# Neighbourhood attention on one core: the layout of attention's output in DRAM, and the order of the transposes of the probabilities

## The chip, the core and the metric

The kernel runs on one core of a Trainium2 chip. The metric is the device time of one execution in microseconds (us); less is better. Three runs of the kernel before took 992.84, 990.8 and 990.86 us, so its median is 990.86 us.

## The reference, cut to what matters

One encoder layer over 2048 tokens (32 rows by 64 columns) of 1024 numbers, all float32:

```
h = rmsnorm(x, norm_0)
q, k, v, gate = split(h @ w_in_0, 4)             # 16 heads of 64
# every query sees 8 rows by 16 columns of keys around it
s = q @ k.T / 8 + bias(rpb_0, row and column offset)
o = softmax(s) @ v
x = x + (o * silu(gate)) @ w_out_0
out = rmsnorm(x, norm_f)
```

## The kernel before, in words

TensorE does the matmuls, and each large product is split into three passes over a high and a low part of the operands. Four stages follow each other on it.

- `stage_one` and `stage_two` project the first and second half of the tokens to q, k, v and the gate. Seven products in place of eight are formed for each block (the method of Strassen), and the results go to DRAM (`qd`, `kd`, `vd`, `sgd`).
- Attention: a loop over 32 cycles, one for each pair of heads p (0 to 7) and quarter of the tokens T (0 to 3), in the order of the list `order` (L1214): T = 1 and 0 for all eight pairs first, then T = 2 and 3.
- `outputs` multiplies the first four row tiles (128 tokens each) by `w_out`, in small pieces between attention's steps.
- `rows_by_seven` multiplies the other twelve row tiles by `w_out`, again by seven products.

One cycle of attention works on two "quads" of columns. `scores` (L1311) makes 64 small matmuls for each quad into two PSUM banks s0 and s1. VectorE adds the bias and takes the row minimum (L1320), ScalarE takes the exponent (L1327), and `normalise` multiplies by the reciprocal of the sum, on GpSimd, ScalarE and VectorE (L1343, L1341, L1339). The probabilities of a cycle lie in eight tiles `X[quad, half, s]`. In the next cycle `turns` (L1347) transposes them on TensorE: 48 transposes of 64 rows, for three blocks b of 120 columns, into two PSUM banks ph0 and ph1 for each block. As soon as a block is done, ScalarE copies ph0 and VectorE copies ph1 to the tile `pta` (L1367, L1365). Then come the scores of the present cycle, then `values` (L1384), which multiplies `pta` by the values `vt` into the bank o, and L1388 multiplies o by the gate into `og`. Between these steps `feed` puts matmuls of the last projections (L384 to L388) or of `outputs` (L1586 to L1590), so that TensorE has work while the other engines do the softmax.

Eight PSUM banks are handed out in turn to whoever asks next; a matmul that opens a bank waits until the bank's last reader is done.

All loads and stores but a few go through one queue, that of SyncE (SP). Eight semaphores take turns there, so an issue waits until the transfer eight issues before it has landed; the transfers are worked off by 16 DMA engines in the order of issue. In each cycle SP issues the loads of the next cycle's keys `kt` (L1232), queries `q` (L1241), values `vt` (L1250), gates `sgt` (L1255) and bias tables `em` (L1269), and stores of the projections. When each is due is written in the code as a count of matmuls (`store`, `later_loads`).

Attention's output passes through DRAM. The tile `og` is 128 partitions (the two heads' 64 dimensions) by 512 tokens, four row tiles i of 128. There is one DRAM tile `ogd[T]` for each quarter, in which each partition holds 16 KB, laid out as row tile, pair, token:

```
ogd = [dram.tile([128, 4, NP, 128], F32, name=f"ogd{T}") for T in range(4)]      # L70
nc.sync.dma_start(ogd[T][:, :, p], og.rearrange("p (i q) -> p i q", i=4))        # L1391
nc.sync.dma_start(t, ogd[T][:, i])                                               # L1418
nc.sync.dma_start(A[m, f]..., ogd[T][:, i, 4 * half:4 * half + 4])               # L1642
```

The 32 stores (L1391, 256 KB each) write four runs of 512 B in each partition. The four loads of `load_og` (L1418, tile `ograw`, 512 KB) read one run of 4 KB, for `outputs`. The 24 loads of `load_rows_of` (L1642, tile `raw`, 256 KB) read one run of 2 KB, for `rows_by_seven`.

In `rows_by_seven` the first three groups of row tiles lead: their products 1 and 2 (six products of 12 matmuls) come first, then product 6 of group 0, which is the first to use the part T2 of `w_out`. T2 is loaded into the tiles `woh` and `wol` by `land_T2` (eight loads of 256 KB, L1610).

Of the kernel before, what the change touches and what calls it, by code (L numbers as in the profile page):

```python
# [24 lines left out]
NP = H // 2  # L25
# [6 lines left out]
RES_BUFS, RES_EARLY = 3, 1  # L32
PLAIN = 4

FRAME, TALL = [0, 4, 12, 17], 15
# [26 lines left out]
def build(ctx, tc, x, xr, xt, wg, bias, w_out, n0, nf, out):  # L62
# [1150 lines left out]
    stored_at = {}  # L1213
    order = [(p, T) for p in range(NP) for T in (1, 0)] + [(p, T) for p in range(NP - 2) for T in (2, 3)]  # L1214
    order += [(NP - 2, 2), (NP - 1, 2), (NP - 1, 3), (NP - 2, 3)]
# [3 lines left out]
    def load_k(p, T):  # L1219
        r0, r1, more = PARTS[T]  # L1220
        base = 12 * (T > 1)
        a, b = r0 * GW, r1 * GW + more
        must(*[("k", p, c) for c in range(a // 512, (b + 511) // 512)])

        def keys():
            if T in (1, 2):
                khalf.clear()
                KT[p, T // 2] = (kp([128, 2048], F32, "kt") if p % 2 == 0 else mkp([128, 1536], F32, "kt"))[:, :1344]
            t = KT[p, T // 2]
            if T == 2:  # L1230
                nc.gpsimd.memset(t[:, 1280:1288], 0.0)
            nc.sync.dma_start(t[:, a - base * GW:b - base * GW], kd[p][:, a:b])  # L1232

        return keys
# [24 lines left out]

    def load_bias(p, T):  # L1260
        fs = []
        kind = BRINGS[T]
        w = 2 * WIDE * TABLES[kind][2]
        EM[p, T // 2, kind] = []
        for quad in range(2):
            t = mp([128, 512], F32, "em")[:, :w]
            EM[p, T // 2, kind].append([t[:, :w // 2], t[:, w // 2:]])
# [30 lines left out]
    def scores(i, between=None):  # L1298
# [16 lines left out]
        for half, (u, n) in enumerate(HALF_ROWS[T]):  # L1315
            xs_ = [by_column(X[quad, half, s], HALF_ROWS[T][half]) for s in range(2)]
            table = EM[p, T // 2, kinds_of[T][half]][quad]
# [29 lines left out]
    def turns(m):  # L1347
# [3 lines left out]
        t = PT[m].rearrange("p (s b n c) -> p b s n c", s=2, b=3, c=64)  # L1351
        for b in range(3):
            ph = [bank(512, f"ph{h}") for h in range(2)]
            at = (2 - b) * k
            for quad in range(2):
                for half in range(2):
                    for s in range(2):
                        for h in range(2):
                            q = slice(64 * h, 64 * h + 64)
                            o = s * 256 + half * 128 + quad * 64  # L1360
                            nc.tensor.transpose(ph[h][:k, o:o + 64], X[quad, half, s][q, at:at + k], ident[q, q])  # L1361
            for h in range(2):
                o, i_ = t[:k, b, :, h::2], ph[h][:k].rearrange("p (s n c) -> p s n c", s=2, c=64)
                if h:
# [6 lines left out]
    def values(m):  # L1371
# [18 lines left out]
        def keep():  # L1390
            nc.sync.dma_start(ogd[T][:, :, p], og.rearrange("p (i q) -> p i q", i=4))  # L1391
            written.add(("og", p, T))
            stored_at[p, T] = clock[0]
# [20 lines left out]
    def load_og(n):  # L1414
        T, i = divmod(n, 4)
        must(*[("og", p, T) for p in range(NP)])
        G[n] = t = wp([128, NK, 128], F32, "ograw")
        nc.sync.dma_start(t, ogd[T][:, i])  # L1418

# [217 lines left out]
    def load_rows_of(m, f, home=None):  # L1637
# [3 lines left out]
        A[m, f] = (home or raw)([128, 512], F32, "raw")  # L1641
        nc.sync.dma_start(A[m, f].rearrange("p (k q) -> p k q", k=4), ogd[T][:, i, 4 * half:4 * half + 4])  # L1642

# [108 lines left out]
    dense, end_of_it = 13.5, 24  # L1752
    amount = [dense] * 25
    first = 16
# [3 lines left out]
    HEAD = 5  # L1758
    amount += [(96 * (12 - len(units_two)) + 48 * PLAIN - sum(amount) - first - end_of_it) / (cycles - 25)] * (cycles - 25) + [end_of_it - 6]
    fill = projections()  # L1760
# [29 lines left out]
    def begin(m):  # L1790
# [11 lines left out]
        if m + 1 < cycles:  # L1802
            nx = order[m + 1]
            later_loads([load_q(*nx), load_k(*nx)], 7, 5)
            later_loads(load_bias(*nx), 3, 1.5)

    stage_one()
# [93 lines left out]
```

## Time and profile before

| | |
|---|---|
| median of three runs | 990.86 us |
| the profiled execution's own time | 991.77 us |
| its span, first to last instruction | 989.8 us |
| TensorE clock granted | 0.998 of full |
| bytes moved by DMA | 227.89 MB in 149228 packets |
| DMA queue of SP | 146096 packets, 71.0% of 16 engines' span |

The page names engines PE (TensorE matmuls), PEld (TensorE weight loads), DVE (VectorE), ACT (ScalarE), POOL (GpSimd) and SP (SyncE, with "q" for its queue). A row of the timeline gives the start and the length in us, engine, line, operation, tile written <- tiles read, the number of instructions merged, and in brackets the idle time before with what ended it. A row of the waits gives who waited for whom: the total in us, how often, and the longest. A row of the table of windows gives the busy time of each engine in a stretch, the granted clock, the share of the 16 DMA engines that was busy, and what they moved in GB/s. PE counts as busy while matmuls overlap, so 39 of 40 slices read 9 tenths or more.

### The profile page before, as it was taken

The numbers are of one execution on the slowest core, as the hardware profiler recorded it, in microseconds if no ns is written. First come the engines' busy times: TensorE is split into PE (matmuls) and PEld (weight loads), VectorE is DVE, ScalarE is ACT, GpSimd is POOL, SyncE is SP. The second block draws the span as 40 slices with busy tenths as digits, with TensorE's granted clock in tenths as the row PEclk, the third lists the DMA queues.
The fourth block names the chain that finished last, engine by engine and source line by source line (L and its number), as shares of the span: only waits on it lengthen the run. The fifth ranks groups of instructions, "written<-read, shape, count | busy, mean of one in ns | idle before, by whom it ended". The sixth has DMA issues, their size and how long they took to land.

```text
span 989.8 us, 22264 instructions
## 1 busy us (share of the span) xinstructions
PE 979.6 (99%) x8172; PEld 797.4 (81%) x8172; DVE 757.3 (77%) x1703; ACT 532.5 (54%) x1310; POOL 148.1 (15%) x396
## 2 busy tenths in 40 slices
PE   9999999999999999999999999999999999999997
PEld 7888888888788888888888777778778777888886
DVE  5899888988565876766776577778878878877866
ACT  7773245465435342333433377677778776653443
POOL 0000001232100000000000033333333332311110
PEclk9999999999999999999999999999999999999999
DMA  8943547777957936657455899988999988997754
GB/s 287 334 131 104 197 130 251 250 224 253 350 179 216 293 117 183 206 165 241 166 184 188 229 275 278 270 260 265 296 287 294 286 227 265 304 369 188 204 148 117
DMA packets 149228, 227.89 MB, mean 230 GB/s; under 512 B 13312, under 2 KB 65792, under 8 KB 149120
## 3 DMA queue, kind: packets, MB, share of 16 engines
q1 hardware_dynamic: 146096, 221.37, 71.0%
q0 software_dynamic: 2592, 4.72, 2.8%
q8 instruction: 64, 1.05, 0.4%
q10 hardware_dynamic: 432, 0.40, 0.1%
q14 instruction: 44, 0.36, 0.1%
HBM read 160.37 MB, written 66.06 MB: 229 GB/s over the span
## 4 chain that ended last, share of the span: by engine, by line
PE 95%; DMA 3%; ACT 1%; DVE 1%; issue 0%; SPq 0%; ACTq 0%
PE pp L440 40%; PE pv L606 13%; PE py L1681 12%; PE o L1384 7%; PE s L1311 5%; PE ph L1361 4%; PE pv L721 2%; PE pp L384 2%; PE pp L388 2%; PE pp L386 2%; DMA kt<-kd 2%; PE po L1586 1%; PE po L1590 1%; PE po L1588 1%; DMA xr<-in_x_dram 1%; ACT x L1327 1%
## 5 line engine op out<-in xcount | busy, mean ns | idle before, releaser
L440 PE MATMUL pp<-h,f 128*128 128x512 f32 x576 | 185.3, 389 | 0.0
L440 PE MATMUL pp<-t,f 128*128 128x512 f32 x702 | 171.4, 389 | 0.0
L440 PEld LDWEIGHTS pp<-t,f 128*128 128x128 f32 x702 | 131.7, 188 | 27.6 <-DVE u L453 0.2
L1327 ACT ACTIVATE x<-x,st 128x253 f32<-128x253 f32 (+1 forms) x256 | 125.1, 496 | 32.9 <-DVE st L1320 32.9
L440 PEld LDWEIGHTS pp<-h,f 128*128 128x128 f32 x576 | 108.1, 188 | 22.6
L440 PE MATMUL pp<-l,f 128*128 128x512 f32 x288 | 112.1, 389 | 0.0
L1343 POOL TENSOR_SCALAR x<-x,st 128x253 f32<-128x253 f32 (+1 forms) x160 | 78.5, 510 | 130.5 <-DVE st L1332 127.1
L1320 DVE CUSTOM_DVE_ANT_0 x<-s,em 128x253 f32<-128x253 f32 (+1 forms) x256 | 87.3, 398 | 6.6 <-issue 4.5
L423 DVE TENSOR_TENSOR f<-raw,f 128x512 fp32r<-128x512 f32 x105 | 75.8, 727 | 20.0 <-ACT f L422 19.9
L1384 PEld LDWEIGHTS o<-pta,vt 120*64 120x64 f32 x1152 | 70.0, 137 | 18.4 <-issue 12.0
L1384 PE MATMUL o<-pta,vt 120*64 120x192 f32 (+2 forms) x1152 | 84.1, 299 | 0.0
L422 ACT ACTIVATE f<-raw 128x512 fp32r<-128x512 f32 x105 | 63.7, 623 | 36.2 <-DVE raw L429 22.0
L1365 DVE COPY pta<-ph 120x512 f32<-120x512 f32 x96 | 60.3, 684 | 13.6 <-PE ph L1361 13.1
L1367 ACT ACTIVATE pta<-ph 120x512 f32<-120x512 f32 x96 | 50.5, 599 | 33.8 <-PE ph L1361 33.6
L440 PEld LDWEIGHTS pp<-l,f 128*128 128x128 f32 x288 | 54.1, 188 | 11.2
L1681 PE MATMUL py<-woh,f 128*128 128x512 f32 x192 | 60.9, 390 | 0.0
L1311 PE MATMUL s<-kt,q 64*32 64x253 f32 (+1 forms) x2048 | 58.7, 362 | 2.2 <-DMA kt<-kd 1.7
L1361 PEld LDWEIGHTS ph<-ident,x 64*120 64x120 f32 x1536 | 47.6, 135 | 11.3 <-issue 10.6
L606 PE MATMUL pv<-wh,t 128*128 128x512 f32 x176 | 56.4, 390 | 0.1
L440 PE MATMUL pp<-sixths,f 128*128 128x512 f32 x198 | 52.7, 389 | 0.0
L461 POOL TENSOR_TENSOR tmp<-tmp,rb 128x512 f32<-128x512 f32 x18 | 28.4, 1580 | 158.0 <-DVE tmp L458 138.3
L1361 PE MATMUL ph<-ident,x 64*120 64x64 f32 x1536 | 52.0, 221 | 0.0
(230 smaller groups left out, 1883.7 us busy)
## 6 DMA issues: line engine op xcount, KB each, us to landing
raw<-in_wg_dram SPq DMA_DIRECT2D x124, 256.0 KB
vt<-vd SPq DMA_DIRECT2D x32, 480.0 KB
row<-in_xr_dram SPq DMA_DIRECT2D x32, 256.0 KB
vd<-v SPq DMA_DIRECT2D x32, 256.0 KB
sgd<-sg SPq DMA_DIRECT2D x32, 256.0 KB
q<-qd SPq DMA_DIRECT2D x32, 256.0 KB
sgt<-sgd SPq DMA_DIRECT2D x32, 256.0 KB
ogd<-og SPq DMA_DIRECT2D x32, 256.0 KB
```

The source lines that it names most:

```text
L422: nc.scalar.activation(t[:, 0], src, AF.Copy)
L423: nc.vector.tensor_tensor(t[:, 1], src, t[:, 0].bitcast(F32), OP.subtract)
L440: nc.tensor.matmul(B[n, P], t[:, int(m == 2), c], x[k][int(m == 1)], start=P in (1, 6, 5) and k == 0 and m == 0, stop=k == 3 and m == 2, s ...
L606: nc.tensor.matmul(p, a[:, o], b, start=P in (1, 6, 5) and k == 0 and m == 0, stop=k == 3 and m == 2, skip_group_check=True)
L1311: nc.tensor.matmul(places[half, s][h * 32:h * 32 + 32], qt[a, g * 64 + half * 32:g * 64 + half * 32 + 32], kt[a, o:o + n * GW].rearrange(" ...
L1320: nc.vector.tensor_tensor_reduce(xs_[s], places[half, s].rearrange("p (r c) -> p c r", c=WIDE), table[s].rearrange("p (c r) -> p c r", c=W ...
L1327: nc.scalar.activation(xs_[s], xs_[s], AF.Exp, bias=st[:, o:o + 1], scale=-1.0, accum_out=st[:, 4 + o:5 + o])
L1343: nc.gpsimd.tensor_scalar(t, t, st[:, o:o + 1], 1.0, op0=OP.mult, op1=OP.mult)
L1361: nc.tensor.transpose(ph[h][:k, o:o + 64], X[quad, half, s][q, at:at + k], ident[q, q])
L1365: nc.vector.tensor_copy(o, i_)
L1384: nc.tensor.matmul(o[s * 64:s * 64 + 64, g0 * 64:g1 * 64], vt[:k, strip, s * 64:s * 64 + 64], moving, start=strip == 0, stop=strip == 7, s ...
L1681: nc.tensor.matmul(B[m, P], t[:, a, c], b, start=P in (1, 6, 5) and k == 0 and i == 0, stop=k == 3 and i == 2, skip_group_check=True)
```

## The change

Two things are changed; what else the diff holds does nothing at the value that it sets.

1. `ogd[T]` is laid out as pair, row tile, token. A store then writes one run of 2 KB in each partition, a load of `load_og` reads eight runs of 512 B, and a load of `load_rows_of` reads four runs of 512 B.
2. `turns` no longer does both quads of a block in a row. With (block, quad), the order is (0,0), (1,0), (0,1), (2,0), (1,1), (2,1), and a block is copied after its quad 1. The pairs of banks are asked for in the same order as before, but those of blocks 1 and 2 are opened eight transposes earlier, and blocks 0 and 1 are copied eight transposes later.

The constant `SHARED` is 0. With it the list `order`, the bias tables loaded, their keys and the tile that holds each pair's keys come out as before, and every row of SyncE, VectorE, ScalarE and GpSimd stands where it stood.

```
+SHARED = 0
...
-    ogd = [dram.tile([128, 4, NP, 128], F32, name=f"ogd{T}") for T in range(4)]
+    ogd = [dram.tile([128, NP, 4, 128], F32, name=f"ogd{T}") for T in range(4)]
...
-        for b in range(3):
-            ph = [bank(512, f"ph{h}") for h in range(2)]
+        ph = {}
+        for b, quad in ((0, 0), (1, 0), (0, 1), (2, 0), (1, 1), (2, 1)):
+            if quad == 0:
+                ph[b] = [bank(512, f"ph{h}") for h in range(2)]
             at = (2 - b) * k
-            for quad in range(2):
-                for half in range(2):
-                    for s in range(2):
-                        for h in range(2):
...
-                            nc.tensor.transpose(ph[h][:k, o:o + 64], X[quad, half, s][q, at:at + k], ident[q, q])
+            for half in range(2):
+                for s in range(2):
+                    for h in range(2):
...
+                        nc.tensor.transpose(ph[b][h][:k, o:o + 64], X[quad, half, s][q, at:at + k], ident[q, q])
+            if quad == 0:
+                continue
...
-            nc.sync.dma_start(ogd[T][:, :, p], og.rearrange("p (i q) -> p i q", i=4))
+            nc.sync.dma_start(ogd[T][:, p], og.rearrange("p (i q) -> p i q", i=4))
...
-        nc.sync.dma_start(t, ogd[T][:, i])
+        nc.sync.dma_start(t, ogd[T][:, :, i])
...
-        nc.sync.dma_start(A[m, f].rearrange("p (k q) -> p k q", k=4), ogd[T][:, i, 4 * half:4 * half + 4])
+        nc.sync.dma_start(A[m, f].rearrange("p (k q) -> p k q", k=4), ogd[T][:, 4 * half:4 * half + 4, i])
```

Where the rows move is TensorE in each of the 32 turns. Before, in turn 10, counted from 0 (tile numbers kept; ph0_7214 and ph1_7215 are the banks of block 0, ph0_7234 and ph1_7235 those of block 1; x tiles up to number 5193 and from 5199 to 5201 are quad 0), from the seventh transpose on:

```order
L1361 MATMUL ph0_7214<-ident_163,x1_5201 120x64 [waits Pool_49]
L1361 MATMUL ph1_7215<-ident_163,x1_5201 120x64
L1361 MATMUL ph0_7214<-ident_163,x0_5195 120x64 [waits Pool_49]
L1361 MATMUL ph1_7215<-ident_163,x0_5195 120x64
L1361 MATMUL ph0_7214<-ident_163,x1_5197 120x64 [waits Activation_49]
L1361 MATMUL ph1_7215<-ident_163,x1_5197 120x64
L1361 MATMUL ph0_7214<-ident_163,x0_5203 120x64 [waits DVE_49]
L1361 MATMUL ph1_7215<-ident_163,x0_5203 120x64
L1361 MATMUL ph0_7214<-ident_163,x1_5205 120x64 [waits DVE_49]
L1361 MATMUL ph1_7215<-ident_163,x1_5205 120x64
L1361 MATMUL ph0_7234<-ident_163,x0_5191 120x64 [waits PE_49]
L1361 MATMUL ph1_7235<-ident_163,x0_5191 120x64 [waits PE_49]
```

The same twelve places of the changed kernel (its block 1 is ph0_7224 and ph1_7225):

```order
L1367 MATMUL ph0_7214<-ident_163,x1_5201 120x64 [waits Pool_49]
L1367 MATMUL ph1_7215<-ident_163,x1_5201 120x64
L1367 MATMUL ph0_7224<-ident_163,x0_5191 120x64 [waits DVE_49,PE_49]
L1367 MATMUL ph1_7225<-ident_163,x0_5191 120x64 [waits DVE_49,PE_49]
L1367 MATMUL ph0_7224<-ident_163,x1_5193 120x64
L1367 MATMUL ph1_7225<-ident_163,x1_5193 120x64
L1367 MATMUL ph0_7224<-ident_163,x0_5199 120x64
L1367 MATMUL ph1_7225<-ident_163,x0_5199 120x64
L1367 MATMUL ph0_7224<-ident_163,x1_5201 120x64
L1367 MATMUL ph1_7225<-ident_163,x1_5201 120x64
L1367 MATMUL ph0_7214<-ident_163,x0_5195 120x64 [waits Pool_49]
L1367 MATMUL ph1_7215<-ident_163,x0_5195 120x64
```

The waits for quad 1's probabilities have moved eight places down. The first two rows of block 1 wait for VectorE and for PE itself, where they waited for PE alone; over the program 62 rows gain such a second wait.

On SyncE the rows stand as before and only the shapes change. Before, at the first two loads of `ograw`:

```order
L1391 DMA ogd0_85<-og_8310 512x1x128 [waits DMAHW2_49,DVE_49]
L1250 DMA vt_8322<-vd0_83 120x1x1024 [waits DMAHW3_49,PE_49]
L1269 DMA em_8313<-in_bias_dram 128x506 [waits DMAHW4_49]
L1418 DMA ograw_8332<-ogd0_85 128x1024 [waits DMAHW5_49,DMAHW2_49]
L1418 DMA ograw_8334<-ogd0_85 128x1024 [waits DMAHW6_49]
L1241 DMA q_8337<-qd1_60 128x512 [waits DMAHW7_49]
L1232 DMA kt_8348<-kd1_68 128x1024 [waits DMAHW0_49]
```

And the same place of the changed kernel:

```order
L1399 DMA ogd0_85<-og_8310 128x512 [waits DMAHW2_49,DVE_49]
L1252 DMA vt_8322<-vd0_83 120x1x1024 [waits DMAHW3_49,PE_49]
L1274 DMA em_8313<-in_bias_dram 128x506 [waits DMAHW4_49]
L1426 DMA ograw_8332<-ogd0_85 128x8x128 [waits DMAHW5_49,DMAHW2_49]
L1426 DMA ograw_8334<-ogd0_85 128x8x128 [waits DMAHW6_49]
L1243 DMA q_8337<-qd1_60 128x512 [waits DMAHW7_49]
L1234 DMA kt_8348<-kd1_68 128x1024 [waits DMAHW0_49]
```

The store has 128 runs in place of 512, each load of `ograw` 1024 in place of 128, and the waits are the same. DMAHW0 to DMAHW7 are the eight semaphores that take turns.

More of the change, by code (lines that the diff above doesn't have):

```diff
@@ L1213, in build @@
     stored_at = {}
-    order = [(p, T) for p in range(NP) for T in (1, 0)] + [(p, T) for p in range(NP - 2) for T in (2, 3)]
+    order = [(p, T) for p in range(SHARED) for T in (1, 0, 2, 3)]
+    order += [(p, T) for p in range(SHARED, NP) for T in (1, 0)] + [(p, T) for p in range(SHARED, NP - 2) for T in (2, 3)]
     order += [(NP - 2, 2), (NP - 1, 2), (NP - 1, 3), (NP - 2, 3)]
@@ L1263, in load_bias @@
         w = 2 * WIDE * TABLES[kind][2]
-        EM[p, T // 2, kind] = []
-        for quad in range(2):
+        got = EM.setdefault(table_at(p, T, kind), [])
+        for quad in range(len(got), upto):
             t = mp([128, 512], F32, "em")[:, :w]
-            EM[p, T // 2, kind].append([t[:, :w // 2], t[:, w // 2:]])
+            got.append([t[:, :w // 2], t[:, w // 2:]])
             o = TABLE_AT[kind] + quad * w
@@ L1316, in scores @@
             xs_ = [by_column(X[quad, half, s], HALF_ROWS[T][half]) for s in range(2)]
-            table = EM[p, T // 2, kinds_of[T][half]][quad]
+            table = EM[table_at(p, T, kinds_of[T][half])][quad]
             for s in range(2):
@@ L1752, in build @@
     dense, end_of_it = 13.5, 24
-    amount = [dense] * 25
+    many = 25
+    amount = [dense] * many
     first = 16
@@ L1758, in build @@
     HEAD = 5
-    amount += [(96 * (12 - len(units_two)) + 48 * PLAIN - sum(amount) - first - end_of_it) / (cycles - 25)] * (cycles - 25) + [end_of_it - 6]
+    amount += [(96 * (12 - len(units_two)) + 48 * PLAIN - sum(amount) - first - end_of_it) / (cycles - many)] * (cycles - many) + [end_of_it - 6]
     fill = projections()
@@ L1805, in begin @@
             later_loads(load_bias(*nx), 3, 1.5)
+            if order[m][0] < SHARED and order[m][1] == 2:
+                later_loads(load_bias(*order[m + 2], 1), 6, 0)
     stage_one()
```

13 lines of the change are left out of this document (7 added, 6 removed).

## The prediction

> **What bounds the kernel now.** I read the page first, then the chain of waits, then who waited on TensorE, then the table of windows and the timeline of SyncE's queue.
>
> ```profile
> span 989.8 us, 22264 instructions
> PE 979.6 (99%) x8172; PEld 797.4 (81%) x8172; DVE 757.3 (77%) x1703; ACT 532.5 (54%) x1310; POOL 148.1 (15%) x396
> ```
>
> TensorE is busy for 979.6 of 989.8 us, so at most 10.2 us are there to be won without taking matmuls away, and this change takes none away. The list of TensorE's waits (engine and line, releaser, us in total, times, longest) says where a part of them lies, and the chain of waits gives the two ends.
>
> ```profile
> PE s L1311 <- DMA kt<-kd: 1.7, 2, 1.4
> PE zp L127 <- DVE z L124: 1.2, 1, 1.2
> PE s L1311 <- PE ph L1361: 0.5, 1, 0.5
> ```
>
> ```profile
> 869.15 114.49 PE py L1681 x504
> 983.67 0.44 DVE y L1446
> ```
>
> The 1.2 us are the start and the 989.8 - 983.7 = 6.1 us after the last product are the end; the change touches neither. In between, 1.7 + 0.5 = 2.2 us of waiting are left, all for the scores (L1311). That is all that a smoother attention can win.
>
> The 1.7 us are two waits for keys, the longer 1.4. Two of the three waits in rows of TensorE's timeline (start, length, the idle time before in brackets):
>
> ```profile
> 733.50 1.94 PE L1311 MATMUL s<-kt,q 64*32 64x253 f32 x64 [0.48 <-PE ph L1361]
> ...
> 809.23 1.94 PE L1311 MATMUL s<-kt,q 64*32 64x253 f32 x64 [1.37 <-DMA kt<-kd]
> ```
>
> The row at 733.50 names PE, but the timeline of SyncE's queue shows that it waited for keys as well:
>
> ```profile
> 720.00 0.57 SPq L1391 DMA_DIRECT2D ogd<-og  x1
> ...
> 725.03 0.81 SPq L1418 DMA_DIRECT2D ograw<-ogd  x2
> ...
> 726.35 0.51 SPq L1232 DMA_DIRECT2D kt<-kd  x1
> ...
> 733.42 0.32 SPq L1232 DMA_DIRECT2D kt<-kd  x1
> ```
>
> The issue at 733.42 is the eighth after the one at 726.35, so it had to wait until those keys had landed, and the scores start at 733.50, right behind. The keys were some 7 us on their way, with two loads of `ograw` ahead of them in the queue. So DMA time inside attention reaches TensorE at three places (the two rows, and a wait of 1.7 - 1.4 = 0.3 us), and elsewhere it is covered.
>
> **The change part by part.** First the price of a run of 512 B. Windows of the trace (busy us and count for PE, PEld, DVE, ACT and POOL, clock, DMA share, GB/s):
>
> ```profile
> 382.50:384.50 2.00, 2.00 (x10) 1.67 (x9) 1.77 (x4) 0.35 (x1) 0.00 (x0) 1.00 0.44 131
> 878.00:886.00 8.00, 8.00 (x37) 6.60 (x36) 7.10 (x12) 4.25 (x9) 0.78 (x1) 1.00 1.05 394
> 595.00:730.00 135.00, 134.67 (x2380) 107.40 (x2377) 103.60 (x374) 100.94 (x321) 47.23 (x169) 1.00 0.90 274
> ```
>
> In the first window one store of values (`vd`, 256 KB in runs of 512 B) is alone: 2 us at 131 GB/s are its 262 KB, and it keeps the sixteen engines busy for 0.44 x 2 = 0.88 us. In the second the queue is full of 256 KB loads with runs of 2 KB: 394 GB/s make 262 / 394 = 0.67 us of each. So 512 B in place of 2 KB costs 0.88 - 0.67 = 0.2 us for 256 KB. For `ograw` (512 KB) I take the same rate for runs of 4 KB: 1.33 us against 1.76, 0.43 us more. Reads in runs of 512 B are not in the trace before. I price them as the store, which is the nearest row; below, the cost cannot be less than none, since the bytes are the same; above, I allow twice the 0.88 us.
>
> In all the 32 stores give back 6.4 us of engine time, and the loads take 24 x 0.2 + 4 x 0.43 = 6.5 us. The engines' total stays, but time moves from the cycles of attention (0.90 busy in the third window) to the four loads of `ograw` and to the end of attention. What counts is who waits there.
>
> [...]
>
> Term 1, the wait of 0.3: in every cycle one store of `og` stands ahead of the keys, as that of 720.00 does. It ends 0.2 us earlier: -0.2, at most the whole 0.3.
>
> Term 2, the keys at 733.50: the two loads of `ograw` ahead cost 2 x 0.43 = 0.86, and the store of 720.00 gives back 0.2, so the wait grows by 0.66. Stores of the cycles before count as well if the queue has not run empty since; each gives 0.2, and three of them would cancel it all. I take the middle: +0.3 (0 to +0.66; if it went all the way in the other direction, -0.48).
>
> Term 3, the wait of 1.37 at 809.23: again one store ahead, -0.2, and up to -0.4 with the next one back.
>
> Term 4, the loads of `raw`. None of attention's cycles lies behind them, but the part T2 of `w_out` does:
>
> ```profile
> 856.27 6.90 SPq L1642 DMA_DIRECT2D raw<-ogd  x6
> ...
> 870.46 0.94 SPq L1642 DMA_DIRECT2D raw<-ogd  x2
> ...
> 873.54 1.39 SPq L1642 DMA_DIRECT2D raw<-ogd  x2
> ...
> 881.55 0.32 SPq L1610 DMA_DIRECT2D wol<-wodT  x1
> ...
> 886.72 0.32 SPq L1610 DMA_DIRECT2D sixths<-wodT  x1
> ```
>
> The last load of T2 is issued at 881.55, and the issue eight later (886.72) tells when it lands. The first product with T2 is the seventh of the chain's 504 matmuls from 869.15, each 114.49 / 504 = 0.227 us; the load is first used by the 83rd matmul, the second of the product's fourth group of three, at 869.15 + 82 x 0.227 = 887.8. That leaves a cover of 1.1 us. Ahead of it are ten loads of `raw`, +2.0, and the stores of two cycles, -0.4: at most 1.6 us later, a stall of 0.5. But the six loads of 856.27 reach over 6.9 us of issuing, where SyncE waits for other things, so part is taken up there. With only the last four and one store (0.8 - 0.2 = 0.6 us) the cover holds. I take 0 (0 to +0.5).
>
> Term 5, the transposes. They are the same 48 with the same pairs of banks in turn. What they could win is a wait for quad 1's probabilities; TensorE's own list of waits has none. What they could cost:
>
> ```profile
> 658.31 1.56 PE ph L1361 x48
> ```
>
> ```profile
> 649.86 1.89 DVE L1365 COPY pta<-ph 120x512 f32<-120x512 f32 x3 [0.92 <-PE ph L1361]
> ...
> 652.29 2.62 PE L1384 MATMUL o<-pta,vt 120*64 120x128 f32 x36
> ...
> 654.50 2.46 POOL L1343 TENSOR_SCALAR x<-x,st 128x184 f32<-128x184 f32 x5 [3.11 <-DVE st L1332]
> ```
>
> A transpose takes 1.56 / 48 = 0.0325 us. Block 0 is complete after 24 in place of 16, so VectorE's three copies begin and end 8 x 0.0325 = 0.26 us later. In these rows of a turn they end at 649.86 + 1.89 = 651.75 and `values` starts at 652.29: the cover of 0.54 us shrinks to 0.28, and nothing is lost. The softmax behind the copies is 0.26 us later too, but quad 1 is asked for 0.26 us later, and quad 0's part on GpSimd ends by 654.50 + 2.46 = 656.96, 1.3 us ahead of the next turn at 658.31. Only the last turn has no scores behind it that cover the copies:
>
> ```profile
> 864.60 1.89 DVE L1365 COPY pta<-ph 120x512 f32<-120x512 f32 x3 [0.95 <-PE ph L1361]
> ...
> 866.53 2.62 PE L1384 MATMUL o<-pta,vt 120*64 120x128 f32 x36
> ```
>
> The copies end at 866.49 and `values` starts at 866.53; 0.26 us later is a loss of 0.2.
>
> Sum: -0.2 + 0.3 - 0.2 + 0 + 0.2 = +0.1 us. The profiled execution took 991.77 us (span 989.8 and 2.0 around it), which is 0.9 above the median of the runs, 990.86; its longest wait for keys alone is 1.37. I put the sum on the median: 990.86 + 0.1, about **991.0 us**. The ends of the terms add up to -0.3 - 0.48 - 0.4 = -1.2 and to 0.66 + 0.5 + 0.2 = +1.4: 989.7 to 992.3.
>
> **The rivals.** A measurement of this kernel tells about 0.2% from no change, 2.0 us: under 988.9 is faster, over 992.8 slower.
>
> (a) 512 B runs cost nothing extra, so that neither stores nor loads change: the three waits stay and only the last turn's 0.2 is left, 991.1. For it speaks that the sum of DMA time stays the same in any case; against it the two windows. [...]
>
> (b) The stores' savings add up from cycle to cycle in a queue that is 0.90 busy, and the keys are early everywhere: 1.7 + 0.5 = 2.2 us go, 990.86 - 2.2 = 988.7, faster. Against it: the `ograw` loads stand right ahead of the second of these waits.
>
> (c) The waits that 62 transposes gain lie on TensorE's path. The list of the transposes' line has them as instructions of its queue:
>
> ```profile
> L1361 PEldq EVENT_SEMAPHORE  x48: 51/51/51, 571.8 to 860.0; - x48
> ```
>
> Before there are 48 of 51 ns each, one or two in a turn, at its head; now two more stand amid the run of 31 turns. If TensorE's queue is not far enough ahead to hide them, 62 x 0.051 = 3.2 us: 994.1, slower. Against it: where a turn has one or two of them the chain gives it 1.56 us all the same (658.31 is one). It decides if a turn takes more than 1.6 us.
>
> (d) Reads of 512 B run at half the store's speed: 1.1 us more for each `raw` and 2.2 more for each `ograw`. The wait at 733.50 grows by 4.4 - 0.2 and T2 lands 10 x 1.1 - 0.4 = 10.6 us late against 1.1 of cover: 4.2 + 9.5 = 13.7, 1004.6. With x us more for each `raw` and 2x for each `ograw` the two places cost 4x - 0.2 and 10x - 1.5, so it is over 2 us from x = 0.26 on. Nothing in the trace speaks for it but that such reads don't occur in it.
>
> **How the numbers follow.** The forecast 0.65, (a) 0.18, (b) 0.07, (c) 0.04, (d) 0.06. The forecast and (a) are within 0.2%: same 0.83; (b) is faster, 0.07; (c) and (d) slower, 0.10. The range holds the forecast's ends and (a), 989.6 to 992.4, rounded outward, and leaves out (b), (c) and (d), 0.17.
>
> **What would show it.** Right: TensorE busy for about 979.6 us again; turns of 1.56 us; the stores' DMA time down and the wait at about 733.5 still there, a little longer; that at about 809 a little shorter; VectorE's copies starting 0.26 us later in a turn. Wrong: turns over 1.6 us (c); products of the last stage waiting for `woh` or `wol` (term 4, d); no wait for keys left at all (b); or a new wait of `values` for the copies in turns other than the last.

## The result, and the profile after

In twenty runs the changed kernel took 997.0 us in the median (992.21 to 1003.42), and the kernel before, in twenty runs beside them, 993.32 us (990.61 to 998.21). The ratio is 1.0035, with a 95% interval of 1.0018 to 1.0051: the change costs 3.5 us, 1.8 to 5.1. The forecast was no change (+0.1 us, 991.0), so it was wrong. Of the 6.0 us between 991.0 and 997.0, 2.3 belong to the reference: the three runs shown first had a median of 990.86, the twenty 993.32. The other 3.7 lie between the two medians; the ratio puts the change at 3.5. That is the subject here.

The profiled execution of the changed kernel took 997.05 us, near the median, with a span of 994.9. That of the kernel before (991.77) was one of its faster ones, so the pair of profiles shows more than 3.5 us. The page after the change, with the row of the queue that fetches instructions:

```profile
span 994.9 us, 22326 instructions
PE 981.2 (99%) x8172; PEld 803.0 (81%) x8172; DVE 754.6 (76%) x1703; ACT 531.9 (53%) x1310; POOL 150.1 (15%) x396
...
q8 instruction: 65, 1.06, 0.5%
```

The span grew by 5.1 us, and only 1.6 of them are in TensorE's busy time (979.6 before). The matmuls are the same 8172; the 62 instructions more are on TensorE's queue. The kernel before has in the same place:

```profile
q8 instruction: 64, 1.05, 0.4%
```

TensorE's waits after the change (engine and line, releaser, us in total, times, longest):

```profile
PE o L1392 <- issue: 2.6, 2, 1.5
PE s L1316 <- DMA kt<-kd: 2.1, 2, 1.8
...
PE s L1316 <- issue: 0.8, 1, 0.8
```

The waits for keys sum to 2.1 us. Before they were 1.7 and, at 733.50, 0.5 more that stood under another name: nothing is gained or lost there. New are 3.4 us of "issue", time in which TensorE waited for nothing that the profile records: neither a semaphore nor a busy engine. A third part does not show as a wait at all. It is found by laying one cycle of each kernel side by side, the same cycle by its shapes. First before, then after (start, length):

```profile
667.39 1.63 PE L1361 MATMUL ph<-ident,x 64*120 64x64 f32 x48
668.94 1.71 PE L1311 MATMUL s<-kt,q 64*32 64x184 f32 x64
670.58 0.66 PE L1384 MATMUL o<-pta,vt 120*64 120x128 f32 x8
```

```profile
669.78 1.62 PE L1367 MATMUL ph<-ident,x 64*120 64x64 f32 x48
671.33 1.76 PE L1316 MATMUL s<-kt,q 64*32 64x184 f32 x64
673.01 0.77 PE L1392 MATMUL o<-pta,vt 120*64 120x128 f32 x12
```

The turn takes 668.94 - 667.39 = 1.55 us before and 671.33 - 669.78 = 1.55 after. But from the start of the scores to that of `values` it is 1.64 us before and 1.68 after: 0.04 us in each cycle are lost inside the scores.

**The loss inside the scores.** A row of 64 scores is both quads of a cycle, 32 recorded matmuls each, and each quad opens two PSUM banks, s0 and s1. Banks are handed out in turn. In the program of either kernel, in all 31 turns with scores behind them, the first quad's s0 waits for no copy of this turn, and its s1 waits for ScalarE's copy of block 0. The second quad's s0 waits for VectorE's copy of block 0, and its s1 for ScalarE's copy of block 1. ScalarE's copies in this turn, before and after:

```profile
668.11 1.09 ACT L1367 ACTIVATE pta<-ph 120x512 f32<-120x512 f32 x2 [0.65 <-PE ph L1361]
...
L1367 ACT ACTIVATE pta<-ph 120x512 f32<-120x512 f32 x96 | 50.5, 599 | 33.8 <-PE ph L1361 33.6
```

```profile
670.73 1.09 ACT L1375 ACTIVATE pta<-ph 120x512 f32<-120x512 f32 x2 [0.91 <-PE ph L1367]
...
L1375 ACT ACTIVATE pta<-ph 120x512 f32<-120x512 f32 x96 | 50.4, 598 | 41.8 <-PE ph L1367 41.7
```

One copy takes 0.60 us. Before, the first ends 668.11 + 0.60 - 667.39 = 1.32 us after the turn's start, 0.23 us ahead of the scores. After, it ends at 670.73 + 0.60 - 669.78 = 1.55, just as the scores start. In the trace ScalarE's semaphore comes at 671.334, and the first matmul into s1 starts at 671.377, where the first into s0 had started at 671.325. The windows of the scores' line alone show it (length, busy us and count for PE and PEld, clock, DMA share, GB/s), first before, then after:

```profile
668.93:668.99 0.06, 0.05 (x8) 0.05 (x12) 1.00 1.11 136
```

```profile
671.32:671.37 0.05, 0.04 (x1) 0.05 (x2) 1.00 0.00 0
671.37:671.42 0.05, 0.05 (x7) 0.05 (x12) 1.00 1.21 163
```

Before, eight matmuls of the scores start within 0.06 us. After, one does, and the others come 0.05 us later. Matmul by matmul, the first into s1 starts 7 ns behind the first into s0 before, and 51 to 52 ns after, in nearly every cycle. In the median over the cycles `values` starts 0.041 to 0.045 us later after the turn's start; over the 31 turns that have scores behind them this sums to 1.3 us. The profile puts it down as busy time, since matmuls into s0, recorded with 0.36 us each in this turn, overlap it.

**The idle of "issue".** TensorE's timeline around two of the three places:

```profile
654.68 0.33 PE L1392 MATMUL o<-pta,vt 120*64 120x192 f32 x1
656.46 0.76 PE L1392 MATMUL o<-pta,vt 120*64 120x192 f32 x7 [1.45 <-issue]
...
722.83 0.59 PE L1392 MATMUL o<-pta,vt 120*64 120x192 f32 x5 [1.15 <-issue]
```

The queue "instruction" of the page says what they are. Its 65 transfers, 1.06 MB in all, are 16 KB each, and TensorE's queue holds 16,622 recorded instructions: 16,622 / 65 = 255.7, so 256 for each transfer. (Before, 16,560 and 64.) The three places, at 597.08, 656.46 and 722.83, lie 8 x 256 and 9 x 256 instructions apart: each at the border of such a block. The transfer that brings the block ends at 595.51, 655.11 and 721.32, and TensorE goes on 1.57, 1.35 and 1.51 us behind it. Before, no border has such a gap. Counted alike in all profiles (the time between two matmuls' starts at a border, less 0.1; what is under 0.26 then is left out), the three sum to 4.2 us.

In attention a transfer of this queue takes 1.1 us in the mean in this trace, and it begins up to 5.7 us behind the border before it.

The sum for the profiled pair, 5.1 us of span: 1.3 inside the scores, 4.2 at borders and -0.1 for the keys. That is 5.4 for 5.1. The borders differ from execution to execution, so the experiments take the parts apart.

### The profile page after: what moved, and what is told of

Same layout as the page of the kernel before. It is cut to its first block, busy times and chain, and to the rows that moved or that the text cites. A ratio compares the mean times of both kernels' runs of the same rounds, so it can differ in the third digit from the quotient of the medians.

```text
span 994.9 us, 22326 instructions
## 1 busy us (share of the span) xinstructions
PE 981.2 (99%) x8172; PEld 803.0 (81%) x8172; DVE 754.6 (76%) x1703; ACT 531.9 (53%) x1310; POOL 150.1 (15%) x396
## 3 DMA queue, kind: packets, MB, share of 16 engines
q8 instruction: 65, 1.06, 0.5%
## 4 chain that ended last, share of the span: by engine, by line
PE 95%; DMA 2%; ACT 1%; issue 0%; SPq 0%; DVE 0%; POOL 0%
PE pp L441 40%; PE pv L607 13%; PE py L1689 12%; PE o L1392 8%; PE s L1316 5%; PE ph L1367 5%; PE pp L385 2%; PE pp L389 2%; PE pp L387 2%; DMA kt<-kd 2%; PE pv L722 2%; PE po L1594 1%; PE po L1596 1%; PE po L1598 1%; DMA land<-in_xt_dram 0%
## 5 line engine op out<-in xcount | busy, mean ns | idle before, releaser
L1316 PE MATMUL s<-kt,q 64*32 64x253 f32 (+1 forms) x2048 | 60.9, 362 | 2.9 <-DMA kt<-kd 2.1
L1367 PEld LDWEIGHTS ph<-ident,x 64*120 64x120 f32 x1536 | 47.4, 134 | 11.3 <-issue 10.6
```

The lines of the kernel that those rows point to most:

```text
L1316: nc.tensor.matmul(places[half, s][h * 32:h * 32 + 32], qt[a, g * 64 + half * 32:g * 64 + half * 32 + 32], kt[a, o:o + n * GW].rearrange(" ...
L1367: nc.tensor.transpose(ph[b][h][:k, o:o + 64], X[quad, half, s][q, at:at + k], ident[q, q])
```

## The experiments

The edits are against the kernel before, unless the changed kernel is named. "Border stalls" are gaps at 256-instruction borders, counted in the one profiled execution of each kernel. All ratios are to the kernel before, run beside.

**The two halves of the change, and two other orders.** e1 has the layout alone, e2 the order alone. e3 and e4 replace the order in `turns`; in e4 a block begins with quad 1, so that the turn's waits stay at its head and no instruction is added.

```
e1: the four lines with ogd as in the change; e2: the loop of turns as in the change
e3: +        for b, quad in ((0, 0), (1, 0), (2, 0), (0, 1), (1, 1), (2, 1)):
e4: +        for b, quad in ((0, 1), (1, 1), (0, 0), (2, 1), (1, 0), (2, 0)):
    +            if quad == 1:      (opens the banks, and skips the copies)
```

> The kernel before with only the new layout of `ogd` (stores of 2 KB, reads of 512 B); the transposes stand as before. Theory B (the order of the transposes costs all: the bank s1 and the position of TensorE's instructions): no change, within 1 us of before, scores' second bank 7 ns behind the first. Theory D (the new DMA shapes make keys and TensorE's instruction blocks late): most of the 3.5 us, 2 to 4 us above before.

> The kernel before with only the new order of the transposes; the layout stands as before. Theory B: the whole loss, 2.5 to 4.5 us above before; of it 32 x 0.045 = 1.4 us because bank s1 waits for ScalarE's copy of block 0, the rest stalls of 1.2 to 1.8 us at each place where TensorE enters a block of 256 instructions that has just landed. Theory D: only the 1.4 us.

> The kernel before with all three blocks' quad 0 first, then the three quads 1; old layout. Block 0 is complete after 32 transposes in place of 24 (changed kernel) and 16 (before). Theory S (the scores' bank s1 opens only when ScalarE's copy of block 0 ends): s1 stands 0.045 + 8 x 0.0325 = 0.30 us behind s0 in each of 32 cycles, 9.6 us above before, plus what instruction stalls add. Rival (the copies have slack and only the extra semaphore waits and stalls count): 107 more waits than before in place of 62, 4 to 6 us.

> The kernel before with the order of the change but quad 1 in place of quad 0 first, (0,1), (1,1), (0,0), (2,1), (1,0), (2,0); old layout. The copies are as late as in the changed kernel, but no semaphore instruction is added: TensorE's queue has as many instructions as before, so its blocks of 256 begin at the same matmuls. Theory S + F (1.4 us from bank s1, the rest from stalls at the moved block borders): 1.4 us above before, s1 0.05 us behind s0. If the moved borders do not count and the order itself makes the stalls: 3 to 4 us as the changed kernel.

| | median us | ratio and interval | border stalls, us |
|---|---|---|---|
| e1_layout | 994.23 | 1.0013 [0.9993, 1.0032] | 1, 1.0 |
| e2_order | 995.04 | 1.0013 [0.9995, 1.0030] | 2, 3.0 |
| e3_late2 | 1028.72 | 1.0345 [1.0309, 1.0381] | 11, 22.5 |
| e4_swap | 998.82 | 1.0050 [1.0027, 1.0073] | 3, 3.9 |

Neither half alone can be told from no change, and neither interval settles its two theories: e1 allows up to 3.2 us, e2 up to 3.0. e4 costs 5.0 us without an added instruction: the 62 waits of the rival (c) are not the price. Its profiled execution was its fastest (995.19 us, span 993.2, 3.4 more than before). It has the late s1 (52 ns) and border stalls, 1.3 + 3.9, less the other waits in attention, which fall from 2.4 to 0.2 us. e3 makes the same two effects large. Its scores and waits:

```profile
674.97 1.63 PE L1362 MATMUL ph<-ident,x 64*120 64x64 f32 x48
676.53 1.99 PE L1311 MATMUL s<-kt,q 64*32 64x184 f32 x64
678.45 1.75 PE L1387 MATMUL o<-pta,vt 120*64 120x128 f32 x24
```

```profile
PE o L1387 <- issue: 10.9, 8, 3.1
PE s L1311 <- issue: 4.6, 1, 4.6
```

From scores to `values` it is 1.92 us in place of 1.64: 0.28 in each cycle, 31 x 0.28 = 8.7. With 22.5 at borders that is 31 of the 35 lost. The rest is the clock: its records have it at half for 3.41 us in four places behind the longest pauses, which costs about 4 x 1.7 = 6.8 us, and the other waits are 1.4 us shorter (the last section has one of the four).

**The place of the loads of values.** The theory was that `vt`, which SyncE issues when a count of TensorE's matmuls is reached, slips from before the keys to behind them and delays both. In g1, g3 and g4 the load is due later, in g2 earlier:

```
-        later_loads([lambda: load_v(*order[m])], 4, 0)
+        later_loads([lambda: load_v(*order[m])], 12.5, 0)    (g1: changed kernel; g3: e3; g4: before)
+        later_loads([lambda: load_v(*order[m])], 3.9, 0)     (g2: before)
```

> The changed kernel with only the load of the values vt (480 KB) moved: behind the keys on SyncE's queue, where it stood right behind the store of og. Theory V (TensorE stalls at a block border when the fetch of its next 256 instructions was asked for after the vt load had been issued, and so waits behind its 480 KB): the stalls go, the 1.4 us of bank s1 stay, and keys come earlier; 3 to 5 us below the changed kernel, at the kernel before within 2 us. Rival P (the stalls depend on the place of the borders alone, which the 62 instructions have moved): as the changed kernel, 3 to 4 us above before.

> The kernel before with only the load of vt moved, ahead of the store of og, so that it is issued 0.6 to 1 us earlier; TensorE's instructions are the same, one by one. Theory V: fetches lose the race more often; 3 to 8 us above before, all of it in stalls at block borders. Rival P: no change, within 1 us of before.

> The kernel with all three quads 0 first (35 us above before), with only the load of vt moved behind the keys. Theory V: only the 32 x 0.30 = 9.6 us of bank s1 and a few stalls are left, 9 to 14 us above before. Rival P: 30 to 36 us above before, as without the move.

> The kernel before with only the load of vt moved behind the keys. Theory V: the stalls that before has in some executions go and the keys come earlier; 1 to 4 us below before, and the executions lie closer together than 990.6 to 998. Rival P: the stalls stay; only the waits for keys (2 us) can go, and the executions spread as before.

| | median us | ratio and interval | border stalls, us |
|---|---|---|---|
| g1_after_vt | 1008.03 | 1.0129 [1.0100, 1.0157] | 3, 3.1 |
| g2_before_early | 1001.52 | 1.0072 [1.0045, 1.0098] | 3, 2.6 |
| g3_late2_vt | 1017.25 | 1.0220 [1.0195, 1.0245] | 10, 11.3 |
| g4_before_vt | 1008.29 | 1.0139 [1.0115, 1.0164] | 2, 3.2 |

The theory failed: both places are worse for the kernel before, and the changed kernel is not mended by the later one and keeps 3.1 us of border stalls. Only e3 gains: g3 has half of its border stalls, 11.3 in place of 22.5, and ends 22 us above before, where the theory had 9 to 14 and its rival 30 to 36. So the place of the load moves the stalls of e3 without being their cause. In the others the times are lost to waits that the change never had, for example in g4:

```profile
PE s L1311 <- DMA kt<-kd: 5.7, 1, 5.7
PE o L1384 <- DMA vt<-vd: 5.4, 2, 4.0
```

**Quieter queues, and block 0 copied first again.** If the instruction fetch is late because it shares the DMA engines with the loads, fewer loads must shrink the border stalls. n1 (before), n2 (changed) and n3 (e3) load each kind of bias table once and `vt` twice and then use these again, so that the bias and the values of later cycles are left out; the instructions of the engines stay. h1 is the changed kernel, layout and all, with block 0 done in one piece.

```
n1, n2, n3: +        if kind in once: (the table loaded first is used again, no load)
            +        if len(vts) > 1: (VT[p, T] is the one of two cycles before, no load)
h1: -        for b, quad in ((0, 0), (1, 0), (0, 1), (2, 0), (1, 1), (2, 1)):
    +        for b, quad in ((0, 0), (0, 1), (1, 0), (2, 0), (1, 1), (2, 1)):
```

> The kernel before without most of attention's loads: the bias tables em are loaded once for each kind and the values vt twice, and every later cycle uses these again (so bias and values of all but the first cycles are left out). TensorE's matmuls are the same. Theory F (late fetches of TensorE's instructions behind other DMA traffic, and late keys): both go, 1 to 4 us below before, and the executions lie closer together. Rival (the stalls at the borders have nothing to do with DMA traffic): as before.

> The changed kernel without the same loads. Theory F with theory S: only the 32 x 0.045 = 1.4 us of bank s1 are left between this run and the kernel before without these loads. Rival: 3 to 4 us between them, as between the changed kernel and before.

> The kernel with all three quads 0 first, without the same loads. Theory F with theory S: 32 x 0.30 = 9.6 us above the kernel before without these loads, of the 35 us that it is above before with them. Rival: 30 us or more.

> The changed kernel with the order (0,0), (0,1), (1,0), (2,0), (1,1), (2,1): block 0 is complete after 16 transposes as before, blocks 1 and 2 are interleaved; no semaphore instruction is added, the new layout stays. Theory S: s1 again 7 ns behind s0, so the 1.4 us are gone: 1.4 to 4 us below the changed kernel, as the layout alone, within 2 us of before. Rival (blocks 1 and 2 interleaved cost as much): as the changed kernel.

| | median us | ratio and interval | border stalls, us |
|---|---|---|---|
| n1_before_calm | 988.87 | 0.9940 [0.9926, 0.9954] | 1, 0.6 |
| n2_after_calm | 993.24 | 0.9988 [0.9975, 1.0000] | 2, 1.7 |
| n3_late2_calm | 1016.87 | 1.0227 [1.0201, 1.0252] | 8, 13.8 |
| h1_block0 | 995.02 | 0.9999 [0.9981, 1.0017] | 3, 2.6 |

e3 gets 11.9 us faster with the quieter queues and its border stalls lose 8.7 us. The times fall short of the theory all the same. n1 gains 6 us where 1 to 4 were expected. n2 stays 4.4 us above n1, as the rival had it (3 to 4) and not the theory (1.4), though its one profile has 1.7 us of stalls in place of 4.2. n3 stays 28 above n1, where the theory had 9.6 and the rival 30 or more. h1 loses nothing. Its cycle reads like that of the kernel before, with 7 ns from s0 to s1 and 1.64 us from scores to `values`:

```profile
666.20 1.62 PE L1367 MATMUL ph<-ident,x 64*120 64x64 f32 x48
667.75 1.71 PE L1316 MATMUL s<-kt,q 64*32 64x184 f32 x64
669.39 0.44 PE L1392 MATMUL o<-pta,vt 120*64 120x128 f32 x4
```

So the late bank doesn't come from the new layout, nor from the early opening of block 2 or the late copy of block 1, which h1 keeps; it comes from the split of block 0. By the times that holds for the whole cost as well, as far as h1's interval (-1.9 to +1.7 us) goes. But the one profile of h1 has border stalls of 2.6 us too, so their number in one execution does not give a kernel's median.

**Is it lateness?** The next theory was that a TensorE held up behind the turn brings the border stalls. k4 makes both engines copy block 0 twice, so that the scores come late in the old order. k1 splits ScalarE's copy of block 0 in two, k3 repeats its copy of block 2, and a2 is the changed kernel once more.

```
k4: +                for _ in range(2 if b == 0 else 1):      (around the two copies)
k1: +                    for j in [slice(0, 1), slice(1, 2)] if b == 0 else [slice(0, 2)]:
    +                        nc.scalar.activation(o[:, j], i_[:, j], AF.Copy)
k3: +                    if b == 2:
    +                        nc.scalar.activation(o, i_, AF.Copy)
```

> The kernel before, its transposes in the old order, with block 0's two copies each made twice, so that they end 0.6 us later. Theory S: bank s1 opens 1.32 + 0.60 + 0.05 - 1.56 = 0.41 us late in each of 32 cycles, 13 us above before. Theory L (a late s1 also makes the fetches of TensorE's instructions late, whatever the order of the transposes): stalls at block borders come on top as in the kernel with three quads 0 first, 30 to 45 us above before. Rival O (the order of the transposes makes the stalls): 13 to 16 us.

> The kernel before with ScalarE's copy of block 0 in two halves, which end 0.24 us later than the whole one. Theory S: s1 about 0.05 us late as in the changed kernel, 1.4 to 1.6 us above before. Theory L: 3 to 5 us above before, as the changed kernel. If late copies do not count at all: no change.

> The kernel before with ScalarE's copy of block 2, the last one, made twice: as much more work for ScalarE as above, and the copies end at 2.9 us of a turn in place of 2.3, but no bank of the scores waits for it and values start at 3.2. Theories S and L: no change, within 1 us of before. If any late copy costs: 1 us or more above before.

> The changed kernel once more. If its stalls at block borders are fixed by where the borders lie, they stand at the same three borders again (after 595.7, 654.7 and 721.4 us), with the same time; if they are a race with the DMA traffic, the stalls stand at other borders and only their sum, some 2 to 5 us, comes again. The scores' second bank is 51 ns behind the first in either case.

| | median us | ratio and interval | border stalls, us |
|---|---|---|---|
| k4_both | 1004.61 | 1.0094 [1.0071, 1.0118] | 0, 0 |
| k1_halves | 994.35 | 0.9996 [0.9975, 1.0017] | 1, 1.3 |
| k3_twice_b2 | 995.34 | 1.0007 [0.9987, 1.0028] | 1, 1.1 |
| a2_after | 996.55 | 1.0019 [0.9996, 1.0042] | 3, 1.5 |

k4 bears on the lateness:

```profile
672.16 1.63 PE L1361 MATMUL ph<-ident,x 64*120 64x64 f32 x48
673.72 2.15 PE L1311 MATMUL s<-kt,q 64*32 64x184 f32 x64
675.80 0.66 PE L1385 MATMUL o<-pta,vt 120*64 120x128 f32 x8
```

```profile
PE s L1311 <- DMA kt<-kd: 1.9, 1, 1.9
```

From scores to `values` it is 2.08 us in place of 1.64, 0.44 more in each cycle and later than e3, and there is no "issue" among TensorE's waits. A late bank costs its own time, 31 x 0.41 to 0.45 = 13 us by the profile. The medians give 9.4 [7.1, 11.7], which is less; part of that may be that the kernel before has a median of 994.25 beside it and a profile of 991.77. Its one profile has no border stalls, and the median leaves no room for them. It also has 61 more semaphore instructions than before, so there is no sign that those bring them. k1 fell short of what it was meant to do: its halves delay s1 by 0.59 us in all, in a few cycles, and can't be told from nothing. a2 repeats the changed kernel with a smaller loss, 1.9 us [-0.4, +4.2], and a profile with 1.5 us at three other borders (662.1, 727.4 and 786.6).

**Quieter still.** n4 (from e3) and n5 (from the changed kernel) load `em`, `vt`, `q` and `sgt` only in the first cycles and use them again, so the later bias, values, queries and gates are left out.

```
n4, n5: as n1, and +            if len(qts) > 1: (QT[p, T] is used again); the same for SG[p, T]
```

> The kernel with all three quads 0 first, with the bias tables, the values, the queries q and the gates sgt loaded only in the first cycles and used again (all later ones are left out); keys, stores and weights stay. The stalls at block borders added up to 23 us in the profile with all loads and to 14 us without em and vt. Theory F (the fetch of TensorE's next 256 instructions waits behind other transfers): with less traffic still, they fall to 5 us or less, and the kernel comes to 998 to 1004 us, 9 us of late bank s1 above the kernel before without loads. Rival O (the order of the transposes holds the fetch back, whatever the traffic): they stay near 14 us, 1013 to 1018 us.

> The changed kernel with the same loads left out. Theory F: its border stalls (4.5 us in the profile with all loads, 2.2 without em and vt) go to 0.5 us or less; 989 to 991.5 us, the 1.4 us of bank s1 above the kernel before without em and vt (988.9). Rival O: they stay at about 2 us, 992 to 994 us.

n4 took 1004.01 us, 1.0102 [1.0071, 1.0134], with 3 border stalls of 3.2 us in all. n5 took 995.0 us, 1.0006 [0.9987, 1.0024], with none, as was expected of the stalls, but it was not as fast as expected (989 to 991.5), and by its time alone the rival (992 to 994) is nearer. Its profile says where. Matmul by matmul against the profile of the kernel before, it is 0.6 us ahead at 863 us and 2.4 behind at 890. The longest wait in between is new:

```profile
PE py L1713 <- ACT f L1679: 1.0, 1, 1.0
```

With n4 there are three doses of the same order of instructions. The windows of attention in e3, n3 and n4 (last but one column: share of the DMA engines that is busy), one fence each:

```profile
595.00:860.00 265.00, 246.50 (x4076) 197.21 (x4071) 184.22 (x648) 175.28 (x551) 80.62 (x289) 0.97 0.81 239
```

```profile
595.00:860.00 265.00, 253.91 (x4327) 203.77 (x4325) 194.97 (x691) 183.44 (x577) 83.18 (x294) 0.99 0.57 161
```

```profile
595.00:860.00 265.00, 262.18 (x4487) 210.99 (x4484) 204.85 (x727) 192.30 (x607) 87.42 (x310) 1.00 0.37 110
```

At 0.81, 0.57 and 0.37 busy the border stalls are 22.5, 13.8 and 3.2 us, and the medians 1028.7, 1016.9 and 1004.0. In the same profiles the fetch begins, in the mean over attention's borders, 3.7, 2.6 and 1.8 us behind the border before it, and takes 1.0 to 1.1 us itself. So what makes it late with busy DMA engines is the time before it begins; that is shown.

**Adding up the profiles.** From the first transpose to the first product of the last stage the profile of the kernel before takes 293.3 us, and the first one of the changed kernel 299.2. Taken off are the border stalls (0 and 4.2) and TensorE's other idle times of over 0.15 us (2.4 and 2.3): 290.9 and 292.7 are left. In the same way e1, h1, k3 and n1, whose block 0 is whole, leave 290.4 to 291.0, and a2, e4, n2 and n5, whose block 0 is split, leave 292.1 to 292.7. So the split costs 1.1 to 2.3 us in each profile, in which the 1.3 of the bank lie, and what else sets two executions apart is stalls and waits. (k1 leaves 291.5, of which 0.6 are its own late bank, and e2 294.2, of which some 1.7 are a slow clock; see the last section.) It also says why h1's stalls of 2.6 us are not seen in its profile's time: its other waits are 0.6 us, where the kernel before has 2.4.

The border stalls of single executions, all loads kept, are 4.2, 1.5, 3.0 and 3.9 us with block 0 split (the changed kernel, a2, e2, e4), and 0, 1.0, 2.6, 1.3 and 1.1 with block 0 whole (the kernel before, e1, h1, k1, k3). The means are 3.1 and 1.2, and they differ by 1.9.

## Why the prediction was wrong, step by step

**Terms 1 to 3, the keys: the sum right by luck.** The forecast summed them to -0.1; in the profiles the waits for keys go from 1.7 + 0.5 to 2.1. But no term came as forecast. Those of 0.3 and 0.48 (at 733.50, which was to grow) are gone, that of 1.37 at 809.23 has shrunk to 0.32 where 0.2 less was forecast, and the longest is new:

```profile
777.01 2.15 PE L1316 MATMUL s<-kt,q 64*32 64x253 f32 x64 [1.77 <-DMA kt<-kd]
...
814.32 1.94 PE L1316 MATMUL s<-kt,q 64*32 64x253 f32 x64 [0.32 <-DMA kt<-kd]
```

The price of runs of 512 B, forecast as +0.2 us for a `raw` and +0.43 for an `ograw`, was about half that. By the distance of landings a `raw` goes from 0.65 to 0.76 us (+0.11) and an `ograw` from 1.24 to 1.48 (+0.24), while an `og` store goes from 0.82 to 0.65. So 0.11 and 0.24 us lie about halfway between the forecast and the nought of rival (a). Both (a) and (d) spoke of this price. (d) fell with it; (a) gave the same time as the forecast and fell with it.

**Term 4, right.** No product of the last stage waits for `woh` or `wol`.

**Term 5, the step that failed.** The prediction put it so: VectorE's copies begin and end 0.26 us later, "the cover of 0.54 us shrinks to 0.28, and nothing is lost". The 0.26 are right: ScalarE's idle time ahead of its first copy goes from 0.65 to 0.91. It asked only one waiter, `values`, which reads what is copied. There is a second, which reads nothing of it: the scores, whose s1 takes over the bank that ScalarE's copy frees. Their cover was ScalarE's, 0.23 us, not VectorE's 0.54, and 0.23 is less than 0.26. The forecast had nought for it; the price is the 0.041 to 0.045 us in each cycle, 1.3 in all, and h1, which gives block 0 its place back and keeps the rest, has 0.9999 where the change has 1.0035. e2, with the order and so the late bank but the old layout, does not contradict it: its +1.3 us [-0.5, +3.0] are this term's size.

The last turn, on the other hand, for which 0.2 us were forecast, costs nothing:

```profile
869.02 1.63 PE L1367 MATMUL ph<-ident,x 64*120 64x64 f32 x48
870.59 0.50 PE L1598 MATMUL po<-wol,gh 128*128 128x512 f32 x1
...
871.71 2.62 PE L1392 MATMUL o<-pta,vt 120*64 120x128 f32 x36
```

The kernel before has its last turn here:

```profile
863.85 1.63 PE L1361 MATMUL ph<-ident,x 64*120 64x64 f32 x48
```

From its start to `values` it is 2.69 us, and 866.53 - 863.85 = 2.68 before. Products of `outputs` lie between, and `values` does not need all copies at once.

**A term that was missing.** The working took TensorE's time outside its listed waits as fixed, since the matmuls are the same. It had no term for the supply of instructions, which the page counts on the same 16 DMA engines (q8, 0.5% of their span after the change) that the prediction found 0.90 busy. In the two profiles of the changed kernel the border stalls are 4.2 and 1.5 us, and in that of the kernel before 0. What is left of the 3.5 us beside the 1.3 of the bank, 2.2 [0.5, 3.8], is of that size, and so is the 1.9 between the means of the four and the five profiles above. That this is all of it in the medians is argued, not shown: these are nine single executions, and they overlap (h1 has 2.6, a2 1.5).

**The rivals.** (c), one of the two that ended slower, had 3.2 us of semaphore instructions. That came near the 3.5 by luck, for another reason. Its list of the transposes' line reads as it said:

```profile
L1367 PEldq EVENT_SEMAPHORE  x110: 51/51/51, 571.1 to 867.0; - x110
```

But its condition was a turn of over 1.6 us, and all turns without a wait for keys take 1.55 to 1.56. (b) fell too: waits for keys remain.

**What stays open.** Why an order that splits blocks brings late fetches. As far as single profiles tell, it isn't lateness behind the turn (k4), added semaphore instructions (e4 has none and stalls, k4 has 61 and doesn't), the place of `vt` alone (g1 keeps its stalls, g3 half of them), or the layout (e1, one stall of 1.0). Which borders stall is plainer: in e3 they lie behind the blocks that TensorE is through with soonest, after 4.1 to 7.0 us where the median block takes 7.9. The kernel before has as many short blocks, but there the fetch begins 2.7 us behind a border in the mean, not 3.7. e3, which opens all six banks of a turn before it copies any, is by far the worst, with 22.5 us; no run here shows why. No version beat the kernel before with its work whole: k1 and h1 are equal to it, and n1 leaves loads out.

## What to carry to other kernels

When a release moves, list every instruction that waits for it, those included that only take the buffer next, and give each engine's copy its own cover: 0.54 us by VectorE was no cover where ScalarE's was 0.23. Idle time that a profile can put down to nothing, at places a multiple of 256 instructions apart, was instruction fetch here, and with the DMA engines some 0.9 busy it moved with the order of TensorE's instructions and from one execution to the next. And three runs of a kernel whose runs spread by 0.8% missed the median of twenty by 2.5 us: the 0.35% of this change were clear of nought with twenty runs of each and were not with twelve (a2).

## What the runs showed of the hardware

A stall at a border does not end with the fetch. In all the stalls counted here TensorE goes on only 1.1 to 1.75 us after the transfer has ended (1.57, 1.35 and 1.51 in the changed kernel). And behind some of the longer pauses the granted clock falls. In e3, behind a pause of 3.05 us (timeline, then windows):

```profile
700.78 1.54 PE L1387 MATMUL o<-pta,vt 120*64 120x128 f32 x12 [3.05 <-issue]
```

```profile
700.80:702.80 2.00, 2.00 (x18) 2.00 (x20) 0.00 (x0) 0.26 (x2) 0.45 (x1) 0.50 0.95 370
702.80:705.00 2.20, 2.20 (x20) 2.03 (x17) 0.14 (x1) 0.00 (x0) 0.00 (x0) 0.73 0.27 98
705.00:708.00 3.00, 3.00 (x14) 2.30 (x13) 2.19 (x6) 1.98 (x4) 0.59 (x1) 1.00 0.40 100
```

The clock is 0.50 right behind the pause; its records have it at half for 3.41 us, from 700.56 to 703.97. In e2 a pause of 1.95 us already did it:

```profile
628.53 3.69 PE L1387 MATMUL o<-pta,vt 120*64 120x64 f32 x26 [1.95 <-issue]
```

```profile
628.50:632.50 4.00, 3.97 (x27) 3.65 (x28) 0.39 (x3) 1.26 (x6) 1.44 (x4) 0.57 0.49 168
```

36 such matmuls take 2.62 us at full clock (the row at 871.71 above), so 26 would take about 1.9 by this estimate; these took 3.69, so the slow clock cost about as much as the pause. The length of the pause alone does not decide. In n3 one of 3.11 us left the clock at 1.00, and one of 2.03 us halved it:

```profile
770.12 1.10 PE L1399 MATMUL o<-pta,vt 120*64 120x128 f32 x16 [3.11 <-ACT x L1339]
...
801.55 1.80 PE L1399 MATMUL o<-pta,vt 120*64 120x192 f32 x14 [2.03 <-issue]
```

```profile
770.10:773.10 3.00, 2.98 (x38) 2.57 (x39) 0.31 (x1) 0.81 (x4) 0.99 (x3) 1.00 0.02 5
802.30:805.70 3.40, 3.40 (x18) 2.78 (x15) 1.52 (x4) 0.75 (x2) 0.78 (x2) 0.50 0.02 5
```
